# Head in eighths with token transposes kept apart from the norm, first SwiGLU in halves, and an expert weight stored by column halves: one DiT layer on one Trainium2 core

## The chip, the cores and the metric

One core of one Trainium2 chip runs one launch of the kernel. The metric is the device time of a run in microseconds. The kernel before was run three times: 1422.38, 1423.0 and 1424.02 us, so the median is 1423.0 us.

## What is computed

One layer of a diffusion backbone in f32 over 256 latent and 256 context tokens of width 1024:

```
mod  = silu(c) @ ada_w + ada_b            # six vectors: shift, scale, gate, twice
u    = rmsnorm(x, norm1_g) * (1 + sc1) + sh1      # and the same for ctx with c_ctx
y    = merge(mLSTM(u @ w_in), diff_attention(u @ w_in)) @ w_out
x    = x + g1 * y
v    = rmsnorm(x, norm2_g) * (1 + sc2) + sh2
x    = x + g2 * sum over the top 4 of 32 experts: gate * (swiglu(v @ w1[e] + b1[e]) @ w2[e] + b2[e])
out  = rmsnorm(x, final_norm_g)
```

SwiGLU is `min(h, 7) * sigmoid(1.702 * min(h, 7)) * (clip(l, -7, 7) + 1)`. Each expert's w1 is 1024 x 2048 and its w2 1024 x 1024, 12 MB together in f32, 384 MB for 32 experts.

## The kernel before, in words

The program is written out in order; each engine and each DMA queue works through its own instructions in the order written. Nearly all loads go through the queue of SyncE (SP), and a load waits there until the buffer that it fills is free.

**Head (lines 201 to 294 and 886 to 905).** The tokens `xm[m]` (m = 0, 1 context, 2, 3 latent) are loaded; ACT and DVE sum their squares (lines 234, 236), `rstd_of` gives 1/rms, and `dg[m]` is the identity times it (line 240). The loop of lines 891 to 905 goes over j = 0 to 3, two blocks k of 128 channels each time. `xpose(k)` multiplies the tokens by `dg`, which turns and scales them in one f32 matmul per 128x128 block, into a bank `xt[k]`. `ada_first(j)` computes 512 columns of the modulation from two quarters of `ada_w1` (1 MB each) in 32 small matmuls that stand in four column groups of 32; ACT copies the result, TensorE turns it (line 266), DVE makes the scale `A1` and the shift `B1`. `u_first` applies them (DVE for even k, ACT for odd k), `u_second` splits u into a rounded part `uh` (ACT) and a rest `ul` (DVE). `first.split(k)` does the same to the weights (`wh`, `wl`), and `first.step(k)` adds uh·wh, ul·wh and uh·wl for the first chunk of the input projection, 12 matmuls of 512 columns. The order in the loop is: two `xpose`, one `step`, two `split`, `ada_first(j)`, `u_first`, `u_second`, one `step`. Steps 6 and 7 of the first chunk follow in the common loop (lines 908 to 920), then the next chunk, the gates (`w_g`, 128 columns wide), with `start_a` in between (small loads; on POOL `trib`, `oneb`, `mng5`, `dng8`; the broadcast of `lam`, line 146).

**Mixer (lines 297 to 905).** The chunks of `w_in`, `w_a`, `w_b` and `w_o` follow in one list of steps, with attention, mLSTM and the second part of the modulation (`sums`, line 311) as generators that advance one tick per step.

**Experts (lines 926 to 1206).** `gather` picks up to 64 tokens for each of two experts with one-hot matrices. `hidden` runs the w1 matmuls (line 1070), then SwiGLU on 128x512 (lines 1081 to 1085; with `parts=2` in two halves of 256), turns the result (line 1090) in bank `ptr` and copies it (line 1091). `between` puts other work there: for the first pair it turns the one-hots of the pair (`transposed`, line 1058), also in `ptr`. `expert` multiplies by w2 (line 1104). The weights stream through slots of 2 MB that reuse the mixer's memory (`epiece`, lines 1006 to 1019); two of them are made of two 1 MB halves.

**The last pair (lines 1235 to 1281).** It keeps both hidden results and multiplies by w2 one half of the output columns at a time (`out_half`): the four calls load, for both experts, half of the rows and half of the columns, which in DRAM are runs of 512 elements (2 KB). `half_gated`, `half_back`, `norm_part` and `norm_end` finish the sum and the last norm and store `out`.

Of the kernel before, what the change touches and what calls it, by code (L numbers as in the profile page):

```python
# [10 lines left out]
F32 = mybir.dt.float32  # L11
# [9 lines left out]
D = 1024  # L21
# [12 lines left out]
HOMES = dict(xc=[0], wk=[1, 2], mk=[3], mv=[4, 5], sums=[6, 7], hm=[8], dk=[1, 3], dv=[2, 4], og=[0], ah=[6], al=[7],  # L34
# [76 lines left out]
def hybrid_layer(ctx: ExitStack, tc, a, out, dbg=None):  # L111
# [102 lines left out]

    load_small("ng1T", "ada_bT")
    sil = sm.tile([128, KT, 32], F32, name="sil")
# [13 lines left out]
    xm = [xc[:, 0], xc[:, 1], x1[:, 0], x1[:, 1]]  # L230
    for m in (2, 3, 0, 1):
        j = f4([128, D], "junk")
        if m % 2 == 0:
            act.activation(j, xm[m], AF.Square, accum_out=ssq[:, m:m + 1])
        else:
            dve.scalar_tensor_tensor(j, xm[m], 1.0, xm[m], op0=OP.mult, op1=OP.mult, accum_out=ssq[:, m:m + 1])
    rs1 = rstd_of(sm, ssq, D, [128, 4], "rs1")
    dg = [t2([128, 128], "dg") for m in range(4)]
    for m in range(4):
        dve.tensor_scalar(dg[m], ident, rs1[:, m:m + 1], None, op0=OP.mult)  # L240

    S0 = ps_s.tile([128, 2, 512], F32, name="S", tag="S")
    A1 = sm.tile([128, 2, KT], F32, name="A1")
    B1 = sm.tile([128, 2, KT], F32, name="B1")
    ng1, abT = small["ng1T"], small["ada_bT"]
    pool.tensor_scalar(abT[:, 1], abT[:, 1], 1.0, None, op0=OP.add)
    quarters = [(j, h) for j in range(4) for h in range(2)]
    aw = {}

    def ada_load(n):  # L250
        for _ in range(n):
            if quarters:
                j, h = quarters.pop(0)
                aw[j, h] = piece(a["ada_w1"][j, h], 8, 256)

    def ada_first(j):
        q = slice(128 * j, 128 * j + 128)
        for h in range(2):
            for kk in range(4):
                k = 4 * h + kk  # L260
                for g in range(4):
                    mm(S0[32 * g:32 * g + 32, 0, q], sil[:, k, :], aw[j, h][:, 2 * kk + g // 2, 128 * (g % 2):128 * (g % 2) + 128],
                       start=(k == 0), stop=(k == KT - 1))
        mod = t2([128, 128], "mod0")
        act.copy(mod, S0[:, 0, q])
        tr(S0[:, 1, q], mod, ident)
        pv = S0[:, 1, q].rearrange("p (g b s) -> p s g b", g=2, b=2)
        c = slice(2 * j, 2 * j + 2)
        over = lambda v: v[:, None, c].to_broadcast([128, 2, 2])
        dve.tensor_tensor(out=A1[:, :, c], in0=pv[:, 0:2, 1], in1=over(abT[:, 1]), op=OP.add)  # L270
        dve.tensor_tensor(out=B1[:, :, c], in0=pv[:, 0:2, 0], in1=over(abT[:, 0]), op=OP.add)
        dve.tensor_tensor(out=A1[:, :, c], in0=A1[:, :, c], in1=over(ng1), op=OP.mult)
# [3 lines left out]
    us, xt = {}, {}  # L276

    def xpose(k):
        xt[k] = pp()
        for m in range(4):  # L280
            mm(xt[k][:, m * 128:(m + 1) * 128], xm[m][:, k * 128:(k + 1) * 128], dg[m], start=True, stop=True)

    def u_first(k):
        us[k] = t2([128, 512], "u")
        for m, s in ((0, slice(256, 512)), (1, slice(0, 256))):
            if k % 2 == 0:
                dve.tensor_scalar(us[k][:, s], xt[k][:, s], A1[:, m, k:k + 1], B1[:, m, k:k + 1],
                                  op0=OP.mult, op1=OP.add)
            else:
                act.activation(us[k][:, s], xt[k][:, s], AF.Identity, scale=A1[:, m, k:k + 1], bias=B1[:, m, k:k + 1])  # L290

    def u_second(k):
        act.copy(uh[:, k], us[k])
        dve.tensor_tensor(out=ul[:, k], in0=us[k], in1=lanes(uh[:, k]), op=OP.subtract)  # L294
# [592 lines left out]
    ada_load(2)  # L887
    first.load(0)
    ada_load(2)
# [500 lines left out]
```

## Time and profile before

| | us |
|---|---|
| three runs, median | 1423.0 (1422.38 to 1424.02) |
| the profiled execution, its own time | 1420.2 |
| its span, first to last instruction | 1418.5 |
| TensorE (PE) busy | 1331.5 (94%) |
| VectorE (DVE) busy | 556.2 (39%) |
| ScalarE (ACT) busy | 288.5 (20%) |
| HBM read over the span | 480.08 MB, 339 GB/s |
| chain that ended last | PE 58%, DMA 31%, DVE 6%, ACT 2% |

A busy PE is not a PE at its peak: matmuls overlap, and their ends are modelled. Shares over the whole span are means over stages with different limits, so the rows below go by stage. In rows of single instructions the columns are start (us), duration (us), engine, line, operation and tiles, count, and in brackets the idle time before it and what ended that. "PEld" is a weight load of TensorE, "SPq" and "ACTq" are DMA issues.

### The profile page before, as it was taken

The numbers are of one execution on the slowest core, as the hardware profiler recorded it, in microseconds if no ns is written. First come the engines' busy times: TensorE is split into PE (matmuls) and PEld (weight loads), VectorE is DVE, ScalarE is ACT, GpSimd is POOL, SyncE is SP. The second block draws the span as 40 slices with busy tenths as digits, with TensorE's granted clock in tenths as the row PEclk, the third lists the DMA queues.
The fourth block names the chain that finished last, engine by engine and source line by source line (L and its number), as shares of the span: only waits on it lengthen the run. The fifth ranks groups of instructions, "written<-read, shape, count | busy, mean of one in ns | idle before, by whom it ended". The sixth has DMA issues, their size and how long they took to land.

```text
span 1418.5 us, 17043 instructions
## 1 busy us (share of the span) xinstructions
PE 1331.5 (94%) x6981; PEld 713.5 (50%) x6981; DVE 556.2 (39%) x1181; ACT 288.5 (20%) x620; POOL 36.2 (3%) x55
## 2 busy tenths in 40 slices
PE   5999999999998999999999999999999999999996
PEld 4778777778988734434434433333332333323332
DVE  3586765686667612222222323222212322123113
ACT  3434334444553311101101101011000100001001
POOL 0030001000010000000000000000000000000000
PEclk9999999999999999999999999999999999999999
DMA  9666343223358799999999999999999999999995
GB/s 361 216 250 231 120 156 119 90 90 113 126 190 360 315 369 410 432 429 430 432 428 431 432 429 431 430 430 432 430 431 431 430 429 433 429 430 432 429 416 198
DMA packets 45070, 482.30 MB, mean 340 GB/s; under 512 B 5619, under 2 KB 5876, under 8 KB 11580
## 3 DMA queue, kind: packets, MB, share of 16 engines
q1 hardware_dynamic: 44268, 479.82, 81.9%
q8 instruction: 57, 0.93, 0.2%
q0 software_dynamic: 432, 0.81, 0.2%
q10 hardware_dynamic: 288, 0.52, 0.1%
q14 instruction: 25, 0.20, 0.0%
HBM read 480.08 MB, written 1.06 MB: 339 GB/s over the span
## 4 chain that ended last, share of the span: by engine, by line
PE 58%; DMA 31%; DVE 6%; ACT 2%; issue 1%; SPq 1%; ACTq 0%; DVEq 0%
PE acc L1070 15%; PE py L1104 9%; PE acc L591 4%; PE acc L593 4%; PE acc L592 3%; PE pga L1036 3%; PE acc L581 3%; PE acc L582 3%; DMA v__6686<-in_w_dram 3%; PE acc L583 3%; DMA v__7709<-in_w_dram 3%; DMA v__7935<-in_w_dram 3%; DMA vA__8179<-in_w_dram 3%; DMA v__6212<-in_w_dram 3%; DMA vA__7138<-in_w_dram 3%; DMA v__7364<-in_w_dram 3%
## 5 line engine op out<-in xcount | busy, mean ns | idle before, releaser
L1081 DVE TENSOR_SCALAR eg<-acc 128x512 f32<-128x512 f32 (+1 forms) x33 | 22.3, 675 | 417.1 <-PE acc L1070 417.1
L1082 ACT ACTIVATE es<-eg 128x512 f32<-128x512 f32 (+1 forms) x33 | 20.4, 617 | 687.8 <-DVE eg L1081 687.8
L568 DVE TENSOR_TENSOR wl<-w,wh 128x512 fp32r<-128x512 f32 (+1 forms) x160 | 106.8, 674 | 85.0 <-ACT wh L567 84.2
L1112 DVE TENSOR_TENSOR Y<-py,g2r 64x512 f32<-64x512 f32 x60 | 41.3, 689 | 239.4 <-PE py L1104 238.7
L591 PE MATMUL acc<-uh,wh 128*128 128x256 f32 (+1 forms) x328 | 109.0, 332 | 0.7 <-ACT wh L567 0.7
L567 ACT CAST wh<-w 128x512 fp32r<-128x512 f32 (+1 forms) x160 | 93.1, 603 | 60.9 <-PE acc L583 28.5
L593 PE MATMUL acc<-uh,wl 128*128 128x256 f32 (+1 forms) x328 | 104.3, 318 | 0.3 <-DVE wl L568 0.2
L592 PE MATMUL acc<-ul,wh 128*128 128x256 f32 (+1 forms) x328 | 104.1, 317 | 0.0
L591 PEld LDWEIGHTS acc<-uh,wh 128*128 128x128 f32 x328 | 61.9, 189 | 12.9 <-ACT wh L567 3.9
L581 PE MATMUL acc<-wh,uh 128*128 128x512 f32 x160 | 65.9, 412 | 0.7 <-DVE gi L348 0.7
L593 PEld LDWEIGHTS acc<-uh,wl 128*128 128x128 f32 x328 | 61.7, 188 | 5.6 <-DVE wl L568 0.7
L592 PEld LDWEIGHTS acc<-ul,wh 128*128 128x128 f32 x328 | 61.9, 189 | 4.4 <-DVE ul L294 0.3
L582 PE MATMUL acc<-wl,uh 128*128 128x512 f32 x160 | 63.6, 398 | 0.0
L583 PE MATMUL acc<-wh,ul 128*128 128x512 f32 x160 | 63.5, 397 | 0.0
L815 PE MATMUL acc<-b1s,cst 128*64 128x512 f32 x256 | 61.7, 604 | 0.0
L1036 PE MATMUL pga<-P,x 128*128 128x128 f32 x512 | 60.1, 275 | 0.4 <-DVE P L938 0.4
L1036 PEld LDWEIGHTS pga<-P,x 128*128 128x128 f32 x512 | 58.5, 192 | 0.6 <-DVE P L938 0.5
L1125 PE MATMUL acc<-Y,PGT 128*128 128x512 f32 x120 | 55.8, 606 | 0.0
L311 DVE SCALAR_TENSOR_TENSOR sums<-w,sil,sums 128x512 f32<-128x512 f32 x56 | 42.5, 774 | 0.0
L1118 DVE TENSOR_TENSOR xs<-xs,acc 128x512 f32<-128x512 f32 x60 | 37.4, 679 | 7.0 <-PE acc L1269 7.0
L1070 PE MATMUL acc<-ws,XG 128*64 128x512 f32 x176 | 39.7, 593 | 0.0
L1125 PEld LDWEIGHTS acc<-Y,PGT 128*128 128x128 f32 x120 | 21.5, 189 | 34.0 <-issue 20.8
(680 smaller groups left out, 2088.2 us busy)
## 6 DMA issues: line engine op xcount, KB each, us to landing
ws<-in_w_dram SPq DMA_DIRECT2D x20, 2048.0 KB, 35.2
w<-in_w_in_dram SPq DMA_DIRECT2D x30, 1024.0 KB, 4.8
w<-in_ada_w_dram SPq DMA_DIRECT2D x24, 1024.0 KB, 5.9
w<-in_w_a_dram SPq DMA_DIRECT2D x4, 1024.0 KB, 4.9
wo<-in_w_o_dram SPq DMA_DIRECT2D x4, 1024.0 KB, 4.9
w<-in_w_b_dram SPq DMA_DIRECT2D x4, 1024.0 KB, 9.2
ws<-in_w_dram SPq DMA_DIRECT2D x3, 1024.0 KB, 13.4
wk<-in_w_in_dram SPq DMA_DIRECT2D x2, 1024.0 KB, 13.4
```

Of the source, the lines that this page charges most:

```text
L567: act.copy(wh[:, 0:n], raw)
L568: dve.tensor_tensor(out=wl[:, 0:n], in0=raw, in1=lanes(wh[:, 0:n]), op=OP.subtract)
L581: mm(self.ps[j], vh[:, k, s], wh, start=st, stop=False)
L582: mm(self.ps[j], vh[:, k, s], wl, start=False, stop=False)
L583: mm(self.ps[j], vl[:, k, s], wh, start=False, stop=sp)
L591: mm(o, wh[:, c], vh[:, k, t0:t1], start=f, stop=False, skip_group_check=g)
L592: mm(o, wh[:, c], vl[:, k, t0:t1], start=False, stop=False, skip_group_check=g)
L593: mm(o, wl[:, c], vh[:, k, t0:t1], start=False, stop=sp, skip_group_check=g)
L1036: mm(p[:, kk, 0:n * CAP], x1[:, tt, k * 128:k * 128 + 128], P[:, tt].rearrange("p e s -> p (e s)"), start=(tt == 0), stop=(tt == 1))
L1070: mm(G[f // 2][64 * (f % 2):64 * (f % 2) + 64], XG[:, k, sw * CAP:sw * CAP + CAP], w[:, f * 512:f * 512 + 512], start=False, stop=(k == KT ...
L1104: mm(Y[r:r + 64], aT_[:, j, fh * 64:fh * 64 + 64], w[:, dh * 512:dh * 512 + 512], start=(kf == 0), stop=(kf == KT - 1))
L1125: mm(p, PGT[parts[dh], 2 * dh + tt, :], Y2[parts[dh], dh], start=True, stop=True)
```

## The change

Five places change. **Head:** raw tokens are turned by plain transposes as soon as they are there (`turn`, copied to `raw` by ACT and DVE); 1/rms is laid out along the columns once (`scale_rows`, in a bank `rsr`); u is made by `u_of`: raw times rsr on DVE, then scale and shift as before. `raw` lies in the two buffers that `mv` takes later. The first modulation goes in eighths of 256 columns: `ada_first(j)` has 16 matmuls and copies the result to `mods[j]`; `ada_turn(j)` turns and folds it in one matmul with `fold`, in a bank of the pair `pp`. **First expert:** SwiGLU in two parts, its pair's one-hots turned in bank `py`, and a one-element Sigmoid on ACT ahead of the loop. **w2:** stored as (column half, row block, 512), so a 2 MB slot holds the two column halves one after the other. **Last pair:** `out_half` loads runs of 2048 elements (8 KB; 4 KB in the last call); `half_gated(1)` and `half_back(1)` work in two parts of 256 columns. **Store:** the first of the four output stores moves from ACT's queue to SP's.

The loop of the head after the change, then the diff cut to what the prediction speaks of:

```diff
+    raw = [b8([128, 4, 512], "raw") for _ in range(2)]
+    def turn(m):
+        for hf in range(2):
+            p = acc()
+            for k in range(4):
+                tr(p[:, k * 128:k * 128 + 128], xm[m][:, (4 * hf + k) * 128:(4 * hf + k) * 128 + 128], ident)
+            dst, src = raw[hf][:, :, m * 128:m * 128 + 128], p.rearrange("p (k t) -> p k t", k=4)
+            (dve.tensor_copy if hf else act.copy)(dst, src)
     for m in (2, 3, 0, 1):
...
+            if m == 3:
+                turn(2)
+                turn(3)
     rs1 = rstd_of(sm, ssq, D, [128, 4], "rs1")
...
+    turn(0)
+    turn(1)
+    pool.tensor_tensor(out=fold, in0=ident[:, 0:64], in1=ident[:, 64:128], op=OP.add)
     def ada_first(j):
+        q = slice(128 * (j % 4), 128 * (j % 4) + 128)
+        for k in range(KT):
+            for b in range(2):
+                g = 2 * (k % 2) + b
+                mm(S0[32 * g:32 * g + 32, 0, q], sil[:, k, :], aw[j][:, k, 128 * b:128 * b + 128],
+                   start=(k < 2), stop=(k >= KT - 2))
+        mods[j] = t2([128, 128], "mod0")
+        act.copy(mods[j], S0[:, 0, q])
+    def ada_turn(j):
+        pt = pp()
+        mm(pt[:, 0:64], mods.pop(j), fold, start=True, stop=True)
+        pv = pt[:, 0:64].rearrange("p (b s) -> p b s", b=2)
+        dve.tensor_scalar(A1[:, :, j], pv[:, 1, 0:2], abT[:, 1, j:j + 1], ng1[:, j:j + 1], op0=OP.add, op1=OP.mult)
+        dve.tensor_scalar(B1[:, :, j], pv[:, 0, 0:2], abT[:, 0, j:j + 1], None, op0=OP.add)
+    def scale_rows():
+        rsr.append(pp())
         for m in range(4):
-            mm(xt[k][:, m * 128:(m + 1) * 128], xm[m][:, k * 128:(k + 1) * 128], dg[m], start=True, stop=True)
+            mm(rsr[0][:, m * 128:m * 128 + 128], ones, dg[m], start=True, stop=True)
+    def u_of(k):
+        u = t2([128, 512], "u")
+        dve.tensor_tensor(out=u, in0=raw[k // 4][:, k % 4], in1=rsr[0], op=OP.mult)
+        for m, c in ((0, slice(256, 512)), (1, slice(0, 256))):
             if k % 2 == 0:
+                dve.tensor_scalar(u[:, c], u[:, c], A1[:, m, k:k + 1], B1[:, m, k:k + 1], op0=OP.mult, op1=OP.add)
             else:
+                act.activation(u[:, c], u[:, c], AF.Identity, scale=A1[:, m, k:k + 1], bias=B1[:, m, k:k + 1])
+        act.copy(uh[:, k], u)
+        dve.tensor_tensor(out=ul[:, k], in0=u, in1=lanes(uh[:, k]), op=OP.subtract)
...
     first.load(0)
+    for _ in range(3):
+        ada_load()
     first.load(1)
+    ada_first(0)
+    scale_rows()
+    ada_turn(0)
+    first.split(0)
+    ada_first(1)
+    u_of(0)
+    first.split(1)
+    ada_load()
+    ada_turn(1)
+    for k in range(KT):
+        if k + 2 < KT:
+            ada_first(k + 2)
+        if k + 1 < KT:
+            u_of(k + 1)
+        ada_load()
+        if k + 2 < KT:
+            first.split(k + 2)
+            first.step(k)
+            ada_turn(k + 2)
...
+    act.activation(warm, ones[0:1, 0:1], AF.Sigmoid)
...
-                        nxt["PGT0"] = transposed(PG, 2)
+                        nxt["PGT0"] = transposed(PG, 2, "py")
...
-            Y = expert(XG, sw, G01.pop(e), w1_of(e), w2p, between, after, gates_turned if (pr, sw) == (LATE, 1) else None)
+            Y = expert(XG, sw, G01.pop(e), w1_of(e), w2p, between, after, gates_turned if (pr, sw) == (LATE, 1) else None, 1 if e else 2)
...
-            nc.scalar.dma_start(rows_of[:, 0:512], xo[:, tt, 0])
+            (nc.scalar if tt else nc.sync).dma_start(rows_of[:, 0:512], xo[:, tt, 0])
...
     def out_half(dh, fh):
-                src = a["w2"][E - 2 + i, fh].rearrange("p (k n) -> p k n", k=4)
-                nc.sync.dma_start(w[i][:, k0:k0 + step], src[:, k0:k0 + step, s])
+                nc.sync.dma_start(w[i][:, k0:k0 + step], a["w2"][E - 2 + i, fh][:, 2048 * dh + k0:2048 * dh + k0 + step])
...
-    half_gated(1)
-    half_back(1)
+    half_gated(1, 2)
+    half_back(1, 2)
```

## Rows read from the trace of the kernel before

**Rows 1.** Busy time by stage: the stretch (us), its length, busy time and instructions of PE, PEld, DVE, ACT and POOL, then the granted clock, the DMA share and GB/s.
```profile
60.00:440.00 380.00, 368.65 (x2129) 305.33 (x2128) 263.26 (x555) 168.54 (x377) 27.70 (x23) 1.00 0.45 161
...
540.00:1340.00 800.00, 764.47 (x3669) 295.05 (x3668) 200.48 (x404) 62.38 (x128) 4.15 (x14) 1.00 1.01 430
...
1370.00:1396.00 26.00, 23.88 (x106) 8.32 (x102) 5.10 (x11) 1.50 (x4) 0.00 (x0) 1.00 1.02 394
```

**Rows 2.** The instructions of the head in order of time (selected), from the tokens' arrival to the sixth step of the first chunk.
```profile
7.15 1.23 DVE L236 SCALAR_TENSOR_TENSOR junk<-x 128x1024 f32<-128x1024 f32 x1 [3.92 <-DMA x<-in_x_dram]
9.67 1.06 ACT L234 ACTIVATE junk<-xc 128x1024 f32<-128x1024 f32 x1 [1.38 <-DMA xc<-in_ctx_dram]
13.05 0.88 DVE L240 TENSOR_SCALAR dg<-cst,rs1y 128x128 f32<-128x128 f32 x4
17.07 1.15 ACT L567 CAST wh<-wk 128x512 fp32r<-128x512 f32 x2 [6.24 <-DMA wk<-in_w_in_dram]
...
23.16 0.48 PE L591 MATMUL acc<-uh,wh 128*128 128x512 f32 x1
23.95 0.40 PE L591 MATMUL acc<-uh,wh 128*128 128x512 f32 x1
24.65 0.39 PE L591 MATMUL acc<-uh,wh 128*128 128x512 f32 x1
...
48.57 0.48 PE L591 MATMUL acc<-uh,wh 128*128 128x512 f32 x1
```

**Rows 3.** One round of the old loop on the chain of waits that ended last (start, us, what).
```profile
36.21 1.93 PE S L262 x64
38.16 0.28 ACT mod L265
38.48 0.33 PE S L266
...
41.62 1.78 PE pp L281 x16
```

**Rows 4.** Groups of instructions of the first 62 us, shapes kept apart: line, engine, operation, tiles, shapes, count | busy us, mean ns of one | idle time before them and what ended it.
```profile
L568 DVE TENSOR_TENSOR wl<-wk,wh 128x512 fp32r<-128x512 f32 x8 | 5.4, 688 | 14.3 <-ACT wh L567 14.3
L294 DVE TENSOR_TENSOR ul<-u,uh 128x512 fp32r<-128x512 f32 x8 | 5.2, 687 | 2.8 <-ACT uh L293 2.8
...
L293 ACT CAST uh<-u 128x512 fp32r<-128x512 f32 x8 | 4.6, 619 | 0.0
L290 ACT ACTIVATE u<-pp,B,A 128x256 f32<-128x256 f32 x8 | 4.1, 562 | 3.5 <-DVE A L272 3.5
L287 DVE TENSOR_SCALAR u<-pp,A,B 128x256 f32<-128x256 f32 x8 | 4.0, 539 | 0.1
...
L309 DVE TENSOR_SCALAR sums<-w,sil 128x512 f32<-128x512 f32 x4 | 1.9, 480 | 0.0
...
L270 DVE TENSOR_TENSOR A<-S,ada_bT 128x4 f32<-128x4 f32 x4 | 0.7, 163 | 5.3 <-PE S L266 4.5 <-issue 0.8
```

**Rows 5.** What hangs on POOL and on `lam`: an instruction in order of time, the broadcast's time from issue to landing, and the instruction of DVE that uses it last.
```profile
43.27 0.77 POOL L146 DMA_DIRECT2D lamr<-in_lam_dram  x1 [0.96 <-PE pp L281]
...
DMA to landing us min/median/max: 4.2/4.2/4.2
...
58.06 0.16 DVE L340 SCALAR_TENSOR_TENSOR nlam<-le 128x1 f32<-128x1 f32 x1 [2.32 <-ACT le L339]
```

**Rows 6.** The first expert between its two weights, in order of time; then as groups (columns as in Rows 4) the first w2 piece of the second expert, and SwiGLU's first instruction at half width in the last pair.
```profile
510.93 1.28 ACT L1082 ACT_TABLE_LOAD   x1 [12.30 <-DVE eg L1081]
513.73 0.63 PE L1090 MATMUL ptr<-cst,el 128*128 128x128 f32 x4 [2.17 <-DVE el L1085]
515.03 5.35 PE L1104 MATMUL py<-v__4796,eaT 128*64 128x512 f32 x16 [0.67 <-ACT eaT L1091]
...
L1104 PE MATMUL py<-v__4928,eaT 128*64 128x512 f32 x16 | 3.6, 592 | 0.0
...
L1081 DVE TENSOR_SCALAR eg<-acc 128x256 f32<-128x256 f32 x2 | 0.8, 420 | 14.4 <-PE acc L1070 14.4
```

**Rows 7.** Two waits of TensorE (the first and last row), and the granted clock (third last column) in two stretches.
```profile
459.99 0.49 PE L581 MATMUL acc<-wh,yh 128*128 128x512 f32 x1 [1.74 <-ACT wh L567]
460.00:462.00 2.00, 1.69 (x4) 1.19 (x5) 1.95 (x4) 0.02 (x1) 0.00 (x0) 0.67 1.00 426
516.00:517.00 1.00, 1.00 (x4) 0.24 (x2) 0.00 (x0) 0.00 (x0) 0.00 (x0) 0.50 1.00 426
1361.18 3.65 PE L1070 MATMUL acc<-vA__8179,XG 128*64 128x512 f32 x16 [1.21 <-DMA vA__8179<-in_w_dram]
```

**Rows 8.** Issues on SP's queue at the first expert, and a stretch of DMA there (columns as in Rows 1).
```profile
520.42 0.33 SPq L1018 DMA_DIRECT2D v__4961<-in_w_dram  x1
527.29 0.33 SPq L1018 DMA_DIRECT2D v__4971<-in_w_dram  x1
...
520.00:530.00 10.00, 10.00 (x48) 3.30 (x46) 1.38 (x2) 0.00 (x0) 0.00 (x0) 1.00 0.82 272
```

**Rows 9.** The end, in order of time: a w2 matmul of the last pair, and two of the stores.
```profile
1396.07 0.64 PE L1259 MATMUL pga<-ws,v__8216 128*64 128x512 f32 x1 [1.06 <-DMA ws<-in_w_dram]
...
1412.08 0.41 ACTq L1230 DMA_DIRECT2D out_dram<-v__8130  x1
1413.29 0.34 ACTq L1230 DMA_DIRECT2D out_dram<-v__8130  x1
```

## What the change will do to the time: the prediction

> **What bounds the kernel now.** I read the busy time by stage first. In the mixer, 60 to 440 us, TensorE (PE) is busy 368.65 of 380 us while DMA works at 0.45 of its share: PE sets the pace. From 540 to 1340 us the DMA engines are full at 430 GB/s and PE follows the weights [rows 1]. So a microsecond won on PE before the weight stream fills is worth one microsecond at the end, as SP's loads wait for buffers that PE frees; once the stream is full, a faster PE is worth nothing; and after the last weights the path is PE again. The change touches the head, the first expert (the stream not yet full) and the last pair.
>
> In order of time, the head's first `step` starts at 23.16 us and its sixth at 48.57 [rows 2]. That is 25.4 us for five, 5.08 us each, though the step's own 12 matmuls take 2.8 us (three start within 0.70 us [rows 2]). The chain of waits shows what else a round of two steps holds on PE: 1.93 us of modulation, 0.28 us waiting for ACT's copy, 0.33 us of turning, 1.78 us of `xpose` [rows 3].
>
> **The head.** PE's cost of one eighth after the change: a step 2.8; half of the old modulation matmuls, 1.93 / 2 = 0.97; one `ada_turn`, which no row shows: at least 0.16, half of the turning's 0.33, at most 0.28 + 0.33 with ACT's copy again on the path [rows 3]; I take 0.3, nearer to the first, since the copy now has a whole step as cover; hand-overs 0.1. Together 4.2 us (4.05 to 4.55). `xpose` is gone from this loop; it returns as 32 plain transposes before it and four matmuls of `scale_rows`.
>
> DVE's and ACT's chain of one eighth, in DVE's order: A1, B1 2 x 0.16; raw times rsr 0.69 (128x512, as the subtractions); scale and shift, on DVE from SBUF between 0.24 (half of the 0.48 of 512 columns) and the 0.54 from PSUM, I take 0.33 each since the 0.48 has the same operands, on ACT 0.56 each; ACT's rounding 0.62; `ul` 0.69; `wl` 0.69 [rows 4]. That is 3.7 with even k and 4.1 with odd k, with hand-overs about 4.2: as long as PE's. So 4.2 us it is, with little slack on either side.
>
> The start. Context tokens are there at 9.67, and three 1 MB pieces later, at 17.07, the first weights: 2.47 us each [rows 2]. PE needs three eighths and those weights before its first step: 9.67 + 4 x 2.47 = 19.5, plus 0.97 is 20.5. DVE's side is later: its copies for the latent tokens stand ahead of its second sum of squares and end when PE has turned 16 blocks, from 7.15 on, in the 1.78 us of as many `xpose` instructions [rows 3] or up to twice that while the clock is still low, and one copy of 0.69 more, so about 11.5; the old 13.05 for `dg` [rows 2] moves to about 14.9. Then dg 0.88, two copies 1.4, and one pass of the chain above, 3.8: 21.0. Old 23.16, so 2.2 us earlier (0.7 to 2.7).
>
> The end. Sixth step at 21.0 + 5 x 4.2 = 42.0, the seventh from 45.1 to 47.9. The eighth waits for its own `ul`: after `ada_turn(7)` at 45.1 come 0.33 + 0.69 + 1.12 + 0.62 + 0.69 and hand-overs, 49.1; then 11 matmuls, 51.7. Before, three steps follow 48.57 without a wait: 57.0. Gain 5.3 us.
>
> A new wait: `mv` takes raw's buffers, so POOL's memsets for it stand until raw is last read, about 46.1, and behind them in POOL's queue `trib`, `oneb`, two small products and the `lam` broadcast. That one needs 0.77 to issue and 4.2 to land [rows 5]: about 52.4 instead of long before. DVE's `nlam` stands ahead of the next chunk's weight splits; it came at 58.06, 1.1 us behind the first chunk's end, and ACT ended its wait [rows 5]; now it comes 1.7 behind. PE has two splits in hand; I charge 0.4 (0 to 2). **Head: -4.9 us** (-1.5 to -6.3). SP's order is nearly the old one; the eighths wait for ring slots that PE frees sooner, at no cost. 32 transposes and their ACT copies lie in the wait for the context tokens and for the first eighths; without that cover they cost 2 x 1.78.
>
> **The first expert.** Its w1 ends some 0.7 us before the table load at 510.93, and its w2 starts at 515.03 [rows 6]. With the Sigmoid's table already there and halves at 0.42 [rows 6], eight DVE instructions take 3.4 us from 510.2, two transposes 0.33, and the first part's copy is done by then: 514.0. The one-hots' copy no longer holds `ptr`. That is 1.0 earlier (0.1 with halves at the 0.54 of [rows 4]). The w2 matmuls of this piece took 5.35 us, of the next expert 3.6 [rows 6]: the granted clock was 0.50, 1.2 GHz, at 516, after 2.17 us in which PE had nothing [rows 6, 7]. The new gaps are 0.4 and 1.3 us; a wait of 1.21 us had no fall behind it, one of 1.74 had [rows 7]. So I take no fall: 1.75 us more, and SP's issue at 520.42 comes 2.7 us earlier. DMA there ran at 272 GB/s for 10 us, so 3.7 us of stream were lost between that issue and the one at 527.29 [rows 8]; the second of them moves by the same 2.7 us but the first gap closes only once. **-2.4 us** (-0.1 to -3.7).
>
> **The last pair.** From 1370 to 1396 us the stream ran at 394 GB/s, against 430 before [rows 1], and this is where the loads have 2 KB runs. At 430 those bytes take 23.8 instead of 26 us, 2.2 us sooner. PE waited for the third of the four loads until 1396.07 [rows 9]; without it the sixteen matmuls end about 1.5 us earlier. **-1.5 us** (0 to -2.2).
>
> The Trainium skill (DMA: Bandwidth & Descriptors, Specifications) puts the least transfer for line rate at 512 B. By that rule runs of 2 KB would cost nothing already and the sum would be 1.5 us smaller; the trace's 394 against 430 speaks otherwise.
>
> **The rest.** The last of ACT's stores is issued at 1413.29 because one issue (0.41) stands between its two products [rows 9]; now SP has it, and SP's own third one follows: -0.3 (0 to -0.45). The halves at the end: PE has the same columns, starts about 0.15 sooner and does the first token block's second half third instead of second: 0 (-0.2 to +0.2). Middle experts load the same bytes in the same slots: 0; a slot of two loads now needs both at its first matmul, and both land long ahead.
>
> **Sum:** 4.9 + 2.4 + 1.5 + 0.3 = 9.1 us. The profiled execution took 1420.2 (span 1418.5), so it would take 1411.1. It stands 2.8 under the median of the runs, 1423.0, so the median would be 1413.9.
>
> **Rivals.**
>
> DVE sets the head. If the SBUF products cost the PSUM price and each of five hand-overs 0.2, the chain is 4.9 us, near the old 5.08, and the head gives 1.4: 1417.4. For it: both chains are equal on paper. Against it: DVE waited 2.8 us in all for ACT at `ul` over eight blocks [rows 4], 0.35 each.
>
> Runs of 2 KB are not what slowed the stream: the last pair gives nothing, 1423.0 - (9.1 - 1.5) = 1415.4. For it: other loads end in those stretches too. Against it: the fall sits just where they run.
>
> The stream swallows it. If the mixer's own waits on loads took back head and first expert, only the end remains: 1423.0 - 1.8 = 1421.2. For it: PE waits for weights' splits in the mixer too, 1.74 before 459.99 [rows 7]. Against it: DMA's share is 0.45 in the mixer [rows 1].
>
> Slower: the clock falls in the head. PE now waits for eighths and for DVE in short pieces; where such a wait passes about 1.7 us, as the one before 459.99 [rows 7], the granted clock goes to 0.5 and the next step costs some 1.75 us more [rows 6]. If that happened at each of eight steps, 14 us would be paid against 9.1: +4.9, 1427.9. It decides at six falls. Against it: after the first step no wait in my order is over 0.5 us. The Trainium skill (TensorE: Matmul & The Clock Gate, HAM oscillation) describes this very pattern, bursts between waits that each start cold; the trace shows single cases, no row a series.
>
> **How the numbers follow.** Forecast 0.58; DVE-bound head 0.14; run length without effect 0.10; a larger gain, at the far bounds of head and first expert (1411), 0.06; swallowed 0.07; slower 0.05. The range reaches from 1410.3, close to all far bounds together, to 1418.8, the DVE-bound case with 1.0 instead of 2.4 us at the first expert. About 0.2% (2.8 us) is what a measurement can tell from no change: the first four cases are faster by more, 0.88; swallowed is within, 0.07; slower 0.05.
>
> **What would show it.** First step near 21 and steps 4.2 us apart; ul of the last block the one wait at the head's end; the gates' chunk starting near 51.7; no table load after 500 us and w2 of the first expert at 3.6 us; above 420 GB/s from 1370 on and no wait in the third load. Steps 4.6 or more apart, or a granted clock of 0.5 in the head, would make the first term wrong; an unmoved weight stream at 540 us, the whole.

## The result, and the profile after the change

The changed kernel takes 1414.51 us (median of 6 runs, 1412.94 to 1415.86) against 1423.5 us (6 runs of the kernel before, 1422.38 to 1424.94): ratio 0.9937 with a 95% interval of 0.9924 to 0.9949, or 9.0 us. The forecast was 1413.9 us, 9.1 under 1423.0. Two more sets of the same changed kernel gave 1413.74 us (ratio 0.9935, 0.9917 to 0.9953) and 1413.61 us (0.9946, 0.9927 to 0.9965). The two profiled executions lie only 5.7 us apart, 1420.2 and 1414.52 us (spans 1418.5 and 1412.9). Where the other 3.3 us are is the main question of the experiments. (In them two single executions, one of e3 and one of e10, took 7745 and 2637 us; they are left out of the ratios, and e3's rows, taken in the first of them, are not used.)

The head after the change, in order of time (columns as in [rows 2], selected). L282 is the modulation (here the third eighth's), L609 the first matmul of a step, L659 the last matmul of the gates' chunk:

```profile
19.86 1.08 PE L282 MATMUL S<-w,sil 128*32 128x128 f32 x32 [0.53 <-DMA w<-in_ada_w_dram]
20.03 0.69 DVE L312 TENSOR_TENSOR ul<-u,uh 128x512 fp32r<-128x512 f32 x1 [0.69 <-ACT uh L311]
20.88 0.49 PE L609 MATMUL acc<-uh,wh 128*128 128x512 f32 x1
25.05 0.50 PE L609 MATMUL acc<-uh,wh 128*128 128x512 f32 x1
...
42.01 0.50 PE L609 MATMUL acc<-uh,wh 128*128 128x512 f32 x1
...
48.85 0.50 PE L610 MATMUL acc<-ul,wh 128*128 128x512 f32 x1 [0.23 <-DVE ul L312]
...
57.21 1.12 PE L659 MATMUL acc<-ones,gate_b 1*128 1x512 f32 x2
```

The first step comes at 20.88 (23.16 before), the sixth at 42.01 (48.57 before): 4.23 us each, 4.17 without the third, which waited for its eighth. The first step stands right behind the third eighth's modulation, and that had waited 0.53 us for its load; on DVE's side `uh` was ready at 20.00 and `ul` at 20.72. The last matmul of the gates' chunk in the kernel before:

```profile
62.84 1.12 PE L641 MATMUL acc<-ones,gate_b 1*128 1x512 f32 x2
```

It comes at 57.21 now, so the head gives 5.6 us.

Groups of the first 57 us (columns as in [rows 4]):

```profile
L282 PE MATMUL S<-w,sil 128*32 128x128 f32 x256 | 8.6, 276 | 1.4 <-DMA w<-in_ada_w_dram 1.4
...
L312 DVE TENSOR_TENSOR ul<-u,uh 128x512 fp32r<-128x512 f32 x8 | 5.5, 693 | 10.2 <-ACT uh L311 10.2
...
L308 DVE TENSOR_SCALAR u<-u,A,B 128x256 f32<-128x256 f32 x8 | 2.9, 410 | 0.1
...
L289 PE MATMUL pp<-fold,mod 128*128 128x64 f32 x16 | 2.7, 253 | 0.4 <-ACT mod L285 0.4
```

`ada_turn` waits 0.4 us for ACT over all eight. DVE waits 10.2 us ahead of `ul`, 1.3 an eighth, and that is its room. POOL and `lam` (answers to [rows 5]):

```profile
46.34 0.11 POOL L664 MEMSET mv<- 128x8 f32 x1 [16.14 <-DVE u L305]
...
47.22 0.76 POOL L146 DMA_DIRECT2D lamr<-in_lam_dram  x1
...
52.44 0.16 DVE L358 SCALAR_TENSOR_TENSOR nlam<-le 128x1 f32<-128x1 f32 x1 [1.34 <-ACT le L357]
```

The memsets wait for raw's last read as forecast, and `nlam` comes at 52.44. No matmul of the gates' chunk waits for it.

The first expert (answers to [rows 6]), and the granted clock (third last column) around the stalls of the mixer and of the first expert:

```profile
494.58 1.28 ACT L1178 ACT_TABLE_LOAD   x1
...
508.43 0.44 PE L1112 MATMUL ptr<-cst,el 128*128 128x128 f32 x2 [0.93 <-DVE el L1107]
510.17 0.62 PE L1112 MATMUL ptr<-cst,el 128*128 128x128 f32 x2 [1.31 <-DVE el L1107]
510.72 5.09 PE L1126 MATMUL py<-v__4853,eaT 128*64 128x512 f32 x16
```

```profile
456.00:463.00 7.00, 6.43 (x16) 4.25 (x15) 3.19 (x5) 2.90 (x6) 0.00 (x0) 0.54 1.01 432
511.00:514.00 3.00, 3.00 (x10) 0.80 (x10) 0.81 (x4) 0.20 (x1) 0.29 (x1) 0.56 1.02 437
```

Both stretches are near 0.5, the 1.2 GHz level. SP's issues around them (answers to [rows 8]), first in the kernel before (two of the mixer, and the one before 520.42 at the first expert), then in the changed one:

```profile
463.77 0.38 SPq L1018 DMA_DIRECT2D v__4820<-in_w_dram  x1
480.83 0.33 SPq L1018 DMA_DIRECT2D v__4830<-in_w_dram  x1
...
511.01 0.33 SPq L1018 DMA_DIRECT2D vB__4951<-in_w_dram  x1
```

```profile
457.77 0.38 SPq L1040 DMA_DIRECT2D v__4877<-in_w_dram  x1
476.76 0.33 SPq L1040 DMA_DIRECT2D v__4887<-in_w_dram  x1
...
506.95 0.33 SPq L1040 DMA_DIRECT2D vB__5008<-in_w_dram  x1
515.85 0.33 SPq L1040 DMA_DIRECT2D v__5018<-in_w_dram  x1
```

The lead is 6.0 us at 457.77 and 4.07 at 476.76: the mixer lost 1.9 us of it between these issues, 18.99 us apart where they were 17.06. Over the first expert the distance is 8.90 where it was 9.41. The end, by stretches of the stream (columns as in [rows 1]) and in order of time (answers to [rows 9]):

```profile
1340.00:1365.00 25.00, 22.87 (x104) 7.45 (x102) 5.34 (x8) 1.22 (x2) 0.00 (x0) 1.00 1.00 430
1365.00:1390.00 25.00, 23.49 (x106) 8.04 (x104) 5.10 (x11) 1.50 (x4) 0.00 (x0) 1.00 0.98 412
```

```profile
1389.89 0.64 PE L1281 MATMUL pga<-ws,v__8273 128*64 128x512 f32 x1 [0.38 <-DMA ws<-in_w_dram]
...
1406.41 0.87 SPq L1257 DMA_DIRECT2D out_dram<-v__8187  x2
...
1406.58 0.38 ACTq L1254 DMA_DIRECT2D out_dram<-v__8187  x1
```

The third load is still waited for, 0.38 us instead of 1.06.

### The profile page after: what moved, and what is told of

It is laid out like the page before. It is cut to its first block, busy times and chain, and to the rows that moved or that the text cites. A ratio compares the mean times of both kernels' runs of the same rounds, so it can differ in the third digit from the quotient of the medians.

```text
span 1412.9 us, 17057 instructions
## 1 busy us (share of the span) xinstructions
PE 1333.1 (94%) x6973; PEld 714.6 (51%) x6973; DVE 564.3 (40%) x1202; ACT 291.9 (21%) x631; POOL 35.3 (3%) x56
## 3 DMA queue, kind: packets, MB, share of 16 engines
HBM read 480.08 MB, written 1.06 MB: 341 GB/s over the span
## 4 chain that ended last, share of the span: by engine, by line
PE 58%; DMA 32%; DVE 6%; ACT 2%; issue 1%; SPq 0%; ACTq 0%; DVEq 0%
PE acc L1092 15%; PE py L1126 9%; PE acc L609 3%; PE acc L611 3%; PE acc L610 3%; PE pga L1058 3%; PE acc L599 3%; PE acc L600 3%; PE acc L601 3%; DMA v__6743<-in_w_dram 3%; DMA v__8165<-in_w_dram 3%; DMA v__8294<-in_w_dram 3%; DMA v__7766<-in_w_dram 3%; DMA v__6269<-in_w_dram 3%; DMA v__7421<-in_w_dram 3%; DMA vA__7195<-in_w_dram 3%
## 5 line engine op out<-in xcount | busy, mean ns | idle before, releaser
L609 PE MATMUL acc<-uh,wh 128*128 128x256 f32 (+1 forms) x328 | 109.1, 333 | 0.7 <-ACT wh L585 0.7
L609 PEld LDWEIGHTS acc<-uh,wh 128*128 128x128 f32 x328 | 61.7, 188 | 14.6 <-issue 4.1
## 6 DMA issues: line engine op xcount, KB each, us to landing
ws<-in_w_dram SPq DMA_DIRECT2D x20, 2048.0 KB, 34.9
```

Source lines behind the costliest of these rows:

```text
L609: mm(o, wh[:, c], vh[:, k, t0:t1], start=f, stop=False, skip_group_check=g)
```

## The experiments

Unless said otherwise each kernel was compared with the kernel before over five rounds, side by side with the others of its set. Set one: e1 to e4 (kernel before 1421.98 us). Set two: e5 to e8 (1422.38). Set three: e9 to e11 (1421.96). Then e12 alone (1423.75). Sets one and two ran on one chip, set three on a second, e12 on a third. A fall, below, is a stretch in which TensorE's granted clock is 0.5.

**The parts alone: e1 to e4.** e1 is the kernel before with the hunks of the head (line 31 to `ada_first` and after, the loop, `ada_w1`). e2 is the kernel before with all other hunks.

> The kernel before with the head's part of the change alone. Theory S (the terms add as forecast: head 4.9, first expert 2.4, last pair 1.5, store 0.3): 4.9 us under the kernel before, so 4.1 to 4.3 us over the changed kernel, about 1418.6. Theory H (the profile after shows the last tail of the gates 5.6 us earlier and all else together at about half a microsecond, so the head is nearly everything): 5.5 to 8.5 us under the kernel before and within 1.5 us of the changed kernel, 1415 to 1416. Theory M (the mixer's low-clock stretch takes back part of what the head gives, as the profile after shows at 456 to 463 us, where 6.0 us of lead became 4.1): about 4 us under, 1419.5, and the low stretch of 6.8 us stands in this profile too, some 5 us later than in the profile before at most.

Measured: 1415.29 us, ratio 0.9948 (0.9930 to 0.9966), 6.7 us under.

> The changed kernel with the old head: first expert, w2 layout, store and halves at the end are changed. Theory S: 4.2 us under the kernel before, about 1419.3. Theory H: 0.5 to 1.5 us under, about 1422.5. Theory M: as S or H at the end, but the low-clock stretch of the mixer lies where it lies in the kernel before (461 to 464.6 us, 3.4 us long), since the old head leaves the mixer's times as they were.

Measured: 1420.65 us, ratio 0.9990 (0.9979 to 1.0001), 1.3 us under. Together 8.0 us, which is the whole within the intervals. The head is most of it (theory H). Of theory M the low stretch in the mixer was right in e1, but e2 fell as long with the old head, against what M had for it (18.97 and 19.06 us between the two issues), so the head doesn't decide it.

e3 is the changed kernel without the first expert's edits:

```
-    warm = mt.tile([1, 1], F32, name="warm")
-    act.activation(warm, ones[0:1, 0:1], AF.Sigmoid)
...
-    nxt["PGT0"] = transposed(PG, 2, "py")
+    nxt["PGT0"] = transposed(PG, 2)
...
-    ... if (pr, sw) == (LATE, 1) else None, 1 if e else 2)
+    ... if (pr, sw) == (LATE, 1) else None)
```

> The changed kernel without the edits at the first expert: no early Sigmoid, whole SwiGLU, the one-hots turned in the old bank. Theory S: 2.4 us slower than the changed kernel, 1416.9, with the first w2 piece starting 1 us later. Theory H: the first w2 piece starts only some 0.2 us later by the profile after (its start moved 4.31 us where the piece before it moved 4.07) and still takes 5.1 to 5.3 us, so 0.2 to 0.5 us slower, 1414.8.

Measured: 1416.34 us (median of seven runs), ratio 0.9962 (0.9946 to 0.9978). For the rows it was run again as e8.

e4 is the changed kernel with the old order of w2:

```
-    nc.sync.dma_start(w[i][:, k0:k0 + step], a["w2"][E - 2 + i, fh][:, 2048 * dh + k0:2048 * dh + k0 + step])
+    src = a["w2"][E - 2 + i, fh].rearrange("p (k n) -> p k n", k=4)
+    nc.sync.dma_start(w[i][:, k0:k0 + step], src[:, k0:k0 + step, s])
...
-    r["w2"] = f(f(i["exp_w2"]).reshape(E, 2, 4, 128, 2, 512).transpose(0, 1, 3, 4, 2, 5)).reshape(E, 2, 128, 4 * D)
+    r["w2"] = rows(f(i["exp_w2"]).reshape(E * D, D), 4).reshape(E, 2, 128, 4 * D)
```

> The changed kernel with the old order of w2 in memory, so the last pair's four loads have 2 KB runs again; the rest of the change stands. If runs of 2 KB are what held the stream at 394 GB/s (theory S): the rate from 1365 to 1390 us falls from 412 to about 394 and the time rises by 0.7 us (the difference of the two profiles at the third load) to 1.5 us (forecast), 1415.2 to 1416. If the run length has no effect (rival): the rate stays at 412 and the time at 1414.5 within 0.3.

Measured: 1414.0 us, ratio 0.9947 (0.9929 to 0.9964): by time no difference that can be told, and not the 1415.2 to 1416 of theory S. The rows show one. The stretch that answers to 1365 to 1390 above, and the third load's wait:

```profile
1365.00:1390.00 25.00, 22.83 (x101) 7.93 (x98) 5.11 (x11) 1.50 (x4) 0.00 (x0) 1.00 1.00 392
```

```profile
1389.18 0.64 PE L1283 MATMUL pga<-ws,v__8273 128*64 128x512 f32 x1 [1.04 <-DMA ws<-in_w_dram]
```

e1, with 2 KB runs too, shows the same wait:

```profile
1392.34 0.64 PE L1281 MATMUL pga<-ws,v__8265 128*64 128x512 f32 x1 [1.06 <-DMA ws<-in_w_dram]
```

From TensorE's last wait on a w1 load to this row are 34.9 us in the three profiles with 2 KB runs (before, e1, e4: 34.89, 34.88, 34.87) and 34.15 to 34.30 in nine with 8 KB runs. So up to this row the run length is worth 0.7 us: S in kind, at its lower end. Less of it reaches the end: from the same wait to the span's end are 57.4 to 57.6 us in the three with 2 KB runs (e4, which has the new stores, 57.38) and 56.7 to 57.2 in the nine with 8 KB, 0.4 less by the means. The rate from 1365 to 1390 us has to be read with the DMA share beside it: divided by the share it is 388 to 394 GB/s in the three with 2 KB runs (before 398 at 1.01, e1 400 at 1.03, e4 392 at 1.00) and 417 to 422 in the ten with 8 KB runs (e6, whose last pair has a change of its own, among them; for instance the changed kernel above 412 at 0.98, e2 426 at 1.01, e5 419 at 1.00, e7 392 at 0.93, e8 400 at 0.95).

**The changed kernel again, twice: e5 and e11.** No edit.

> The changed kernel once more, for its time beside the others on this chip and for a second profile. If the gap between the two gains (9.0 us by the medians, 5.7 us by the profiled executions) is the chance of one execution, that is where and for how long the granted clock falls to 0.5 at 190, 455 and 511 us, then this profile has the same head (21, then 4.2 us an eighth) and the same places of falls, but lengths that differ by multiples of about 3.4 us, and its runs spread over 4 us or more in step with the mean clock; median 8 to 9 us under the kernel before. If the falls were fixed by the kernel, their lengths would be those of the first profile (3.4, 6.8, 3.4).

Measured: 1413.74 us, runs 1411.72 to 1415.59. The profile has the same places of falls, and one more, in the head; the windows row is of 17 to 22 us:

```profile
17.00:22.00 5.00, 4.62 (x67) 3.46 (x68) 3.58 (x9) 1.42 (x4) 0.00 (x0) 0.50 1.02 428
```

```profile
21.74 0.80 PE L609 MATMUL acc<-uh,wh 128*128 128x512 f32 x1
...
26.71 0.50 PE L609 MATMUL acc<-uh,wh 128*128 128x512 f32 x1
```

The first step comes 0.86 us later than in the first profile and takes 4.97 instead of 4.17 us; the gates' last matmul is at 58.59 instead of 57.21. That the kernel alone doesn't fix it is shown by the first profile and by e11.

> The changed kernel on the same chip as the two with fillers: 8 to 9 us under the kernel before, runs over 3 to 4 us; a third profile of it, with falls at 190 and 511 us, and at 456 and 17 us in some executions only.

Measured: 1413.61 us, runs 1410.29 to 1417.39. The profiled execution was the fastest, 1410.29 us, and the expectation was wrong for it: the clock stands at 1.00 at 17 to 22, at 190, in the mixer and at the first expert. Windows, SP's issues and the first w2 piece of e11:

```profile
456.00:463.00 7.00, 5.84 (x24) 4.55 (x25) 4.31 (x7) 3.70 (x7) 0.00 (x0) 1.00 0.99 422
511.00:514.00 3.00, 3.00 (x16) 1.01 (x14) 0.00 (x0) 0.00 (x0) 0.00 (x0) 1.00 1.02 437
```

```profile
457.46 0.38 SPq L1040 DMA_DIRECT2D v__4877<-in_w_dram  x1
474.40 0.33 SPq L1040 DMA_DIRECT2D v__4887<-in_w_dram  x1
...
504.60 0.33 SPq L1040 DMA_DIRECT2D vB__5008<-in_w_dram  x1
511.85 0.33 SPq L1040 DMA_DIRECT2D v__5018<-in_w_dram  x1
```

```profile
508.16 3.65 PE L1126 MATMUL py<-v__4853,eaT 128*64 128x512 f32 x16
```

The mixer's distance is 16.94 us where it was 18.99 with the fall, the first expert's 7.25 where it was 8.90, and the stretch from the gates' last matmul to a load issue past the fall at 190 us is 0.6 shorter. Most of that 0.6 is given back before the mixer's first issue, where e11 is ahead by 0.3 (457.46 against 457.77). Together 0.3 + 2.05 + 1.65 = 4.0 us; the two executions differ by 4.2. So one kernel shows or doesn't show each fall, though the stalls are the same to 0.02 us (0.93 and 1.31 us before the two pairs of transposes in both). Nor does the chip alone decide it: on the chip of the first two sets the mixer, the same code in all of them, fell in e1, e2 and e5 and not in e4, e7 and e8.

**Does TensorE or DVE set the head? e7.** Half of each eighth's modulation products are left out, the rest is the changed kernel:

```
-        for k in range(KT):
+        for k in range(KT // 2):
             for b in range(2):
...
-                   start=(k < 2), stop=(k >= KT - 2))
+                   start=(k < 2), stop=(k >= KT // 2 - 2))
```

> The changed kernel, which leaves out half of the modulation's products: each eighth's 16 matmuls on TensorE become 8 (the loads, and all that DVE and ACT do, stay as they are). Theory P (TensorE alone sets the 4.17 us of an eighth and DVE has room): steps 3.7 us apart and the first chunk's end some 3 us earlier. Rival D (DVE's chain and its hand-overs are as long as TensorE's, as forecast): steps stay at 4.0 to 4.2 us, the head's end at most 1 us earlier. Rival L (the loads of the eighths, 1 MB at 430 GB/s, 2.4 us each with the first weights between them, set the first three): a wait on the load of w grows at the third to fifth eighth. In time: 3 us faster than the changed kernel by P, under 1 us by D.

Measured: 1413.41 us, ratio 0.9936 (0.9919 to 0.9954), the changed kernel's time within 0.3. The steps of its profile:

```profile
29.19 0.51 PE L609 MATMUL acc<-uh,wh 128*128 128x512 f32 x1
...
32.93 0.51 PE L609 MATMUL acc<-uh,wh 128*128 128x512 f32 x1
...
46.94 0.51 PE L609 MATMUL acc<-uh,wh 128*128 128x512 f32 x1 [0.44 <-ACT uh L311]
```

They stand 3.74 us apart, 0.43 less: TensorE sets the 4.17, and DVE and ACT have room down to 3.74 at least. Theory P named the bound and overrated what it gives at the end. The first interval was 4.85 us with a clock fall at 19 to 23 us, the last eighth waits for ACT, and the gates' last matmul comes at 56.02, 1.2 us earlier instead of 3. In the time even that drowns.

**The first expert once more: e8** (the edit of e3).

> The changed kernel without the edits at the first expert, a second time, beside the changed kernel on the same chip and for a profile of it. By the forecast's term 2.4 us slower than the changed kernel; by the first comparison of the two profiles 0.2 to 0.5 us slower. If the term is real although the start of the first w2 piece hardly moved, it must lie in the granted clock: with the longer stall (2.2 us before the transposes) the fall at 512 us is longer here (6.8 us or more) than with halves (3.4 us).

Measured: 1416.38 us, ratio 0.9959 (0.9944 to 0.9974). By the means of the runs, 1416.33 (8) against 1413.78 (6), it is 2.6 us slower than the changed kernel, +-1.8 (95%). SP's issues over the first expert, 9.41 us apart as in the kernel before:

```profile
505.25 0.33 SPq L1040 DMA_DIRECT2D vB__5000<-in_w_dram  x1
514.66 0.33 SPq L1040 DMA_DIRECT2D v__5010<-in_w_dram  x1
```

In e1, which has the old form too, the clock stayed low for longer:

```profile
506.43 0.33 SPq L1040 DMA_DIRECT2D vB__5000<-in_w_dram  x1
517.15 0.33 SPq L1040 DMA_DIRECT2D v__5010<-in_w_dram  x1
```

That is 10.72 us. With halves the distance was 8.65 to 8.91 in five profiles (the first, e2, e4, e5, e7) and 7.25 in e11. So halves give 0.5 us where both fall alike, and the old form fell for longer in one of its three profiles. The expected explanation (always longer) is not borne out by e8 itself; that the rest of the 2.6 us is such longer falls is likely, not shown.

**Filling the stalls: e6, e9, e10, e12.** Idle matmuls go into a bank that is overwritten before anyone reads it. In the mixer, before the third step of the first w_o chunk:

```
+        if ch is chunks[-2] and k == 2:
+            pf = pp()
+            for _ in range(7):
+                mm(pf, br["yh"][:, 0, 0:128], two(br["yh"], 0), start=True, stop=True)
         ch.step(k)
```

and in `hidden` before each pair of transposes (e6: 4 and 9 of 256 columns against `g2r`; e9: 3 and 3 of 128, in `expert` only):

```
         for i in range(parts):
+            for _ in range(3 if fill else 0):
+                mm(pt_[:, 256:384], ident, ident, start=True, stop=True)
```

> The changed kernel with idle matmuls (into a bank that nobody reads before it is overwritten) in two stalls of TensorE: 7 of 512 columns in the 1.74 us before the third step of the first w_o chunk (454 us), and 4 + 9 of 256 columns before the two pairs of transposes of the first SwiGLU (508 and 510 us). Theory F (the clock falls because of these stalls, and what they cost reaches the end): no fall to 0.5 at 455 to 463 and at 511 to 516, the first w2 piece at 3.6 instead of 5.1 us, the mixer's stretch 1.7 to 3.4 us shorter; 3 to 5 us faster than the changed kernel, and a smaller spread of runs. Rival (the stream or a later wait takes it back): the falls go but the time stays within 0.5 us. Rival 2 (the falls have nothing to do with the stalls): falls at the same places.

Measured: 1418.72 us, ratio 0.9970 (0.9959 to 0.9982), 5 us slower than the changed kernel. The falls at 455 and 511 us are gone (16.96 us between the mixer's issues, first w2 piece 3.65), but the fillers were mis-sized, and they ran in the last pair too, which has halves as well:

```profile
508.96 4.15 PE L1115 MATMUL ptr<-g2r,cst 128*128 128x256 f32 x18 [0.51 <-ACT eaT L1119]
...
1383.25 4.15 PE L1115 MATMUL ptr<-g2r,cst 128*128 128x256 f32 x18 [0.46 <-ACT v__8294 L1119]
```

Nine fillers took 4.15 us in a gap of 1.31, and waited for ACT's read of the other half of their bank. At the first expert the distance became 11.0 us; in the last pair 3.4 us more stood on the path (60.6 instead of 57.2 us from TensorE's last wait on a w1 load to the span's end).

> The changed kernel with idle matmuls in the same two stalls, cut to the gaps and kept out of the last pair: 7 of 512 columns before the third step of the first w_o chunk, and in the first expert alone 3 + 3 of 128 columns (0.24 us each by the run before). Theory F: no fall at 455 to 463 us (17.0 us between the two issues around it instead of 19.0) and none at 511 us (first w2 piece 3.6 us), no loss in the last pair now; 1.5 to 3.5 us faster than the changed kernel, 1410.5 to 1412.5, and a narrower spread of runs. Rival T (the stream takes it back): both falls gone, the time within 0.5 us of the changed kernel's 1413.8 to 1414.5.

Measured: 1412.26 us, runs 1409.96 to 1412.7, ratio 0.9929 (0.9911 to 0.9947). The first expert, where the second fillers still held the transposes back a little (7.79 us between the issues):

```profile
507.14 0.94 PE L1115 MATMUL ptr<-cst 128*128 128x128 f32 x6 [1.09 <-ACT eaT L1119]
508.23 3.65 PE L1132 MATMUL py<-v__4867,eaT 128*64 128x512 f32 x16
```

e10 adds nine fillers of 128 columns to the head (4 before `scale_rows`, 2 before `ada_first(1)`, 1 before `ada_turn(1)`, 2 before `ada_first(2)`), into the half of S that nothing uses now:

```
+    def busy(n):
+        for _ in range(n):
+            mm(S0[:, 1, 0:128], ident, ident, start=True, stop=True)
```

> As the one before, and idle matmuls of 128 columns in the stalls of the head before the first step: 4 before the broadcast of rs, 2 before the second eighth's modulation, 1 before its turn, 2 before the third eighth's. Theory F: no fall to 0.5 at 16 to 24 us in any profile, the first steps stay 4.2 us apart, and the mean falls by 0.3 to 0.7 us more, as half of the executions that were profiled had that fall (first two steps 4.97 instead of 4.17 apart, first step 0.9 later: 1.4 us). Rival: the fillers delay the work on the path, the first step comes 0.3 us later than 21 and nothing is gained.

Measured: 1411.79 us (median of five runs, 1409.93 to 1413.13); ratio 0.9929 (0.9909 to 0.9948). First step at 20.55, no fall in the head: no loss, and no gain that can be told.

e12 is e10 without the fillers before the second pair of transposes.

> As the kernel with fillers in the head, the w_o chunk and the first expert, but in the first expert only the three before the first pair of transposes: those before the second pair waited 1.09 us for ACT's read of the bank and held the second pair back (7.79 us between the two issues of loads around it, against 7.25 in the one profile of the changed kernel without a fall, and 8.9 with one). If the first stall (0.93 us) is what brings the fall there, or the mixer's falls before it do: no fall, 7.2 to 7.3 us, 0.5 us faster than with all fillers, about 1411.4. If the second stall (1.31 us) is enough: 8.9 us with a fall, about 1 us slower, 1413.

Measured: 1411.21 us (4 runs, 1410.42 to 1414.34), ratio 0.9916 (0.9890 to 0.9941). The time can't tell it from e10. The profile, of the slowest of the four, does:

```profile
509.15 0.41 PE L1126 MATMUL ptr<-cst,el 128*128 128x128 f32 x2 [1.31 <-DVE el L1119]
509.49 5.35 PE L1140 MATMUL py<-v__4873,eaT 128*64 128x512 f32 x16
```

The fall is back (8.95 us between the issues): in this profile the 1.31 us stall sufficed, without the first one.

What the fillers show, over all usable profiles (a fall is a granted clock of 0.5 right behind the stall):

| Stall | As in the kernel | Filled |
|---|---|---|
| mixer, 1.74 us before the third w_o step | 5 of 9 fell | 0 of 4 (e6, e9, e10, e12) |
| first expert | 8 of 9 fell (all but e11) | 0 of 3 (both gaps: e6, e9, e10), 1 of 1 (first gap alone: e12) |
| head, 0.4 to 1.4 us before the first step | 3 of 9 fell (new head: e5, e6, and e7 with half the modulation) | 0 of 2 (e10, e12) |

No fall came behind a stall that was filled, but the table mixes chips. At 190 us, where no kernel has fillers, ten of these 13 profiles fell, and the three that did not are e9, e10 and e11, the set on the second chip; e11, without a filler, fell neither in the mixer nor at the first expert. So e9 and e10 can't tell fillers from that set. Their second fillers also came behind 1.09 us of idle time (the row above) and so did not fill that gap. Without this set the first expert fell in 8 of 8 profiles as it stands, in 0 of 1 with both gaps filled (e6) and in 1 of 1 with the second open (e12); the mixer in 5 of 8 against 0 of 2, the head in 3 of 7 against 0 of 1. That the falls come from the stalls is likely for the first expert, on two profiles, and open for the mixer and the head.

e9, e10 and e12 have the lowest ratios; beside the changed kernel of the same set (1413.61) e9 and e10 are 1.35 and 1.8 us lower in the medians, inside the intervals. Their lowest runs and e12's (1409.9 to 1410.5) are about the changed kernel's own best (1410.29 in e11), so the fillers show no lower floor; whether they keep the kernel nearer to it, the intervals don't tell.

## Why the prediction was right, and where it was not

**The total** was 9.1 and came out at 9.0 (8.6 and 8.4 in the two later sets), but not by the sum of its terms, as three sizes were off. By the rows the parts give 5.9 (head), 0.5 (first expert, where both kernels fall alike), at most 0.7 (last pair) and 0 (store), 7.1 in all. The other 1.3 to 1.9 us have no place in the rows; longer falls of the old form at the first expert are the likely one, as below. That the total was met so closely is in part luck.

**The head** (-4.9; measured -5.6 between the first two profiles, -5.9 from the mean of two profiles with the old head to the mean of the eight in which the new head stands unaltered, 63.14 to 57.2). The path came out as told in most of its steps: the period (4.2, 4.17 when no eighth is late), the seventh at 45.05, the eighth's `ul` as the one wait at the end, at 48.85. The start came out in time (21.0, 20.88) but not in its cause: "DVE's side is later" failed. DVE was done at 20.72, and the first step followed the third eighth, for whose load TensorE waited until 19.86 where the forecast had 19.5. And the two chains are not equal, as the forecast had them "with little slack on either side": TensorE binds (e7). The rival in which DVE sets the head is out: DVE's scale and shift from SBUF cost 0.41 us each by the mean and not 0.54, and its idle time ahead of `ul` is 10.2 us over eight blocks. (Its sum was too small, too: with 0.54 twice and five hand-overs of 0.2 the chain of an even k is 5.1 us, not 4.9, the old period, and the rival stood at 1418.4.) The charge of 0.4 for `lam` was not due: `nlam` does end 1.0 us behind the first chunk, but no matmul waits for it, so the two splits in hand seem to cover it. That is 0.4 of the 0.7 to 1.0 that the head gave beyond the forecast.

**The first expert** (-2.4; measured 2.6 +- 1.8 in time, 0.5 in the rows). The size came out about right for a wrong reason. The start of w2 was to come 1.0 us earlier by the halves; against `eg` it came 0.25 earlier (4.62 us from `eg` to w2, before 4.87). The step that failed is "eight DVE instructions take 3.4 us": from 506.10 to the end of the last at 510.02 they took 3.9, with a 0.43 wait for the second bank of w1's sums and hand-overs between. And "I take no fall" failed in five of six profiles with halves: a stall of 1.31 us was enough in e12, although [rows 7] had one of 1.21 without a fall. Those 1.65 us, not the start, are what is still to be had here, as e11's 7.25 shows. How 2.7 us became the term's 2.4 the forecast did not work out.

**The last pair** (-1.5; measured -0.7). Measured up to the third load; 0.4 is left at the span's end. The run length is the cause, and the rival without effect is out by e4's rows, if not by its time: 388 to 394 GB/s at full share with 2 KB, 417 to 422 with 8 KB, for the same bytes. The mis-sized step is "without it the sixteen matmuls end about 1.5 us earlier": the wait of 1.06 fell to 0.38, it did not vanish. The Trainium skill (DMA: Bandwidth & Descriptors, Specifications) puts the least transfer for line rate at 512 B. These rates differ from that: between 2 and 8 KB the rate still rose.

**The store** (-0.3; measured 0). ACT's last issue does come 0.53 us earlier (16.69 us behind the third load's row, before 17.22), but SP's own, now behind one more, ends at 1406.41 + 0.87 = 1407.28, 17.39 behind it, and is the last; ACT's ended 17.56 behind it before (17.22 + 0.34). Nothing in the span answers to it: from the third load to the span's end it is 22.5 to 23.0 us in the profiles with the new stores and 22.5 and 22.7 in the two with the old. The step that failed is the 0.3 itself: SP's third issue was put behind the moved one, and its end was not worked out.

**The gap between medians and profiles.** The mixer's fall lasted longer in the changed kernel's first profile than in the kernel before's (18.99 against 17.06 us between the same two issues, and 16.94 without a fall). Taken out, the pair of profiles differs by 5.7 + 1.9 = 7.6 us. The other 1.4 us lie within what runs of one kernel differ by; which falls they hold can't be read from unprofiled runs.

**The slower rival** (a fall at each of eight steps) is out, but its seed is real: in three of nine profiles of the new head (one of them e7's) the clock fell once, around the last waits ahead of the first step, and e5 paid 1.4 us for it. It did not repeat: behind the first step no wait is over 0.4 us (0.44 in e7), as the prediction had it. That this is the reason is not shown. The rival in which the stream swallows the gains is out by e1: 6.7 us of head alone arrive at the end.

The Trainium skill (TensorE: Matmul & The Clock Gate, Part 1) says that the number of matmuls which run at the low clock at a kernel's start varies from run to run of the same kernel. The traces show the like in the middle of one: the same w2 piece took 5.09, 5.03 and 3.65 us in three executions of the changed kernel.

## What to carry to other kernels

Ask of a stall of TensorE like these of 1.3 and 1.7 us what the clock may do behind it, and price it as a chance: here 1.65 to 2 us in more than half of the profiles, so that the gain between one pair of profiles was off by 3.3 us from that of the medians while each row was exact. Compare profiles stage by stage, between two events that both kernels have (two issues of the same loads), and take out the stages where the granted clock differs before a term is called measured. When an issue is moved to another queue, compute the end of the queue that receives it. Before fillers are called the cause of a quiet clock, look at a stall that none of the kernels fills: here it told the chip's set from the fillers.

## What the hardware showed beyond the forecast

The stall of 1.74 us in the mixer cost 0.1 us in the kernel before, with a low clock of some 3.4 us behind it (17.06 against 16.94), and 2.05 in the changed one with some 6.8: where nothing fell, the work behind that stall waits for ACT again (0.94 to 0.96 us before the fourth step), and the short fall is paid out of that wait, which is gone in the kernel before. In e1, e6, e7 and e9 to e11 the clock also fell for 3.4 to 6.8 us between 861 and 875 us, in e11 behind waits for weights of 1.2 us at most. There the stream sets the pace: from the issue after the first expert's w1 to TensorE's last wait on a w1 load are 839.6 to 840.9 us in these six and 839.7 to 840.8 in the others.
